# One core, a streaming encoder layer: additions of squares on VectorE, and background steps moved out of the v projection

## The chip, the cores and the metric

The program runs on one core of a Trainium2 chip. The metric is the device time of one execution in microseconds (us). The kernel before takes 2237.66 us, the median of three runs that lie between 2231.12 and 2242.47.

## The reference

One layer works on a prompt of 2048 tokens and a sample of 64 tokens, each with its own conditioning vector. The model width is 1024, the feed-forward width 2816.

```python
mod = c_act @ w_ada + b_ada                       # six vectors: sh1, sc1, gt1, sh2, sc2, gt2
h = rmsnorm(x, g1) * (1 + sc1) + sh1
u, q, k, v, o, gates = split(h @ w_in)            # 512 columns each, and 8 gates
pool_out = pool_mixer(u)                          # causal means over 2, 4, 8, 16 rows, 4 groups
hs = mlstm(q, k, v, gates)                        # 4 heads, chunks of 64 rows
hs = headnorm(hs) * sigmoid(o)
x = x + gt1 * (concat(pool_out, hs) @ w_out)
h2 = rmsnorm(x, g2) * (1 + sc2) + sh2
conv = causal_depthwise_conv3(h2 @ w_up)          # a and g, 2816 columns each
x = x + gt2 * ((silu(g) * a) @ w_down)
y = rmsnorm(x, g_final)
```

All data are float32. The final states of the pooling, the memory and the convolution are outputs too.

## The kernel before

The work has two halves. The **attention half** goes through four token groups of 512 columns (the fourth has 576, with the sample). Channels lie on the partitions, tokens along the free dimension. A float32 product is made from three passes of rounded pieces: a weight or an activation is split into a high part (ScalarE, `act.activation(..., AF.Copy)`, line 359) and the rest (VectorE, a subtraction, line 362). Weights that were split in group 0 are written to memory (`hl_kept`) and in groups 1 to 3 are read back whole (line 348), in pieces of 512 KB. The **feed-forward half** goes through three groups of 704 columns and uses sums of up-projection weights (`wsum`) that the attention half has to prepare.

In each attention group the stages are: `proj_v` (the v projection with the gates, line 1038), then for each of four heads the q, k and o projections (`proj_qko`, each one `gemm` of 24 matmuls, line 415) with the previous head's memory work (`lstm`, lines 1176 to 1254) placed between their matmuls, then four u projections with the pooling mixer, then the output projection (`outproj`), whose rows go to `x2d` and into a sum of squares.

Work that belongs to later stages is written as Python generators in five lists `bg[0]` to `bg[4]`. `tick(i)` lets the first generator of list i take one step; the places of `tick` in the matmul loops set where in the program that step's instructions stand. Four kinds of step matter here.

- **Modulations**, `ada(m, False)` in `bg[3]`, one vector of 1024 values for each of groups 1, 2 and 3 (`gt1` is made in group 0). Sixteen steps each multiply one 128 x 512 piece of `w_ada` with the conditioning vectors and add it up on VectorE (lines 194 and 196), and issue the load of a later piece (line 181), three pieces ahead, into one of four `raw` tiles. Then a few matmuls (lines 204, 211) turn the sums into columns.
- **Weight sums**, `up_sums` in `bg[4]`, over groups 1 to 3: 44 units of 512 KB. A unit is loaded by two transfers (line 801), four additions on VectorE (lines 824, 825, 827, 828) turn it into the sums, and one transfer (line 811) stores it. Each unit takes four steps. There are four tiles, so the load of unit i + 2 reuses the tile of unit i - 2 and has to wait until that was stored.
- **The norm of the next group**, `norm1` in `bg[1]`: ScalarE squares each of the eight row blocks (line 846) and GpSimd adds them up (line 848). In the last group `norm_h` (lines 675 to 695) stands in its place and prepares the feed-forward half's input.
- **The second norm's sum**, `sq_acc` in `outproj`: after each of the eight output rows (line 578 adds the residual, line 580 stores it) ScalarE squares it (line 449) and GpSimd adds it (line 450).

In the first part of group 0 and in the feed-forward half the order of PE, ACT, DVE and POOL is the program's own. Elsewhere a scheduler may issue an instruction ahead of its place once its inputs and tiles are there; transfers marked with `keep_in_program_order` (those of `up_sums` among them) keep their order among each other. Nearly all transfers are issued by one queue, SP, in order: a transfer that waits for a tile or for its data holds the ones behind it. Each engine's own instructions run in order as well.

Of the kernel before, what the change touches and what calls it, by code (L numbers as in the profile page):

```python
# [12 lines left out]
ALU = mybir.AluOpType  # L13
# [46 lines left out]
def tile_layer(ctx: ExitStack, tc: tile.TileContext, xT, vecs, cst, rst, rowv, w_mod, w_ada, w_qkou, w_v, w_pool,  # L60
# [39 lines left out]
    def tick(i=0):  # L100
        q = bg[i]
        while q:
            try:
                next(q[0])
                return
            except StopIteration:
                q.pop(0)
# [297 lines left out]
    def gemm(ps, W, mv, o, ks=None, order=None, late=None, ups=(1, 3, 4, 6)):  # L405
        order = order or list(range(len(mv)))
        ks = ks or order
        for k in ks:
            if late is not None and k == late:
                drain(0, 2)  # L410
            at = order.index(k)
            U = W.at(at // 4)
            for pi, (a, b) in enumerate(PASSES):
                for bi, (lo, hi) in enumerate(o.blks):
                    pe.matmul(ps[bi][:, :hi - lo], U[:, a, k % 4 * P:(k % 4 + 1) * P], mv[k][:, b, lo:hi],  # L415
                              start=(at == 0 and pi == 0), stop=(k == order[-1] and pi == 2))
            if at in (1, 2, 4, 6, 7):
                tick(0)
            if at in ups and not quiet:
                tick(4)  # L420
            if at == 3 and o.last and not spare:
                tick(1)
            if at == 4 and not quiet and not spare:
                tick(3)
            if spare and at in (1, 3, 4, 6):
                tick(1)
        for i in (1, 3):
            tick(i)
        for gen in list(bg[2]):
            if next(gen, 0) == 0:  # L430
                bg[2].remove(gen)
# [12 lines left out]
    def sq_acc(ssum, src, T, first):  # L444
        if first:
            act.activation(ssum[:, :T], src, AF.Square)
        else:
            s = scr()
            act.activation(s[:, :T], src, AF.Square)
            pool.tensor_tensor(out=ssum[:, :T], in0=ssum[:, :T], in1=s[:, :T], op=ALU.add)  # L450

    def ssum_tile():
        return sp.tile([P, TMAX], F32, tag="ssum", name="ssum", bufs=1)
# [154 lines left out]
    class Sums:  # L608
# [14 lines left out]
        def load(self, nm):  # L623
            for j in range(2):
                t = self.make(nm, j)
                r = 0
                for v in t:
                    b, n = r % 2, v.shape[1]
                    nc.sync.dma_start(out=v.bitcast(F32), in_=Bd[BN.index(nm), 2 * j + r // 2, :, b:b + n])
                    r += n  # L630
# [158 lines left out]
    if True:  # L789
# [6 lines left out]
        def up_sums():  # L796

            def load(f, c):
                w = a1.tile([P, 4, 256], F32, tag="w4", name="w4", bufs=4)
                for i in range(2):  # L800
                    tc.keep_in_program_order(nc.sync.dma_start(out=w[:, 2 * i:2 * i + 2, :], in_=w_up[NF * i + f].rearrange(
                        "p (h c) -> p h c", h=2)[:, :, c:c + 256]))
                return w
            todo = [(f, c) for f in range(NF) for c in (0, 256)]
            pin = tc.keep_in_program_order
            nx = [load(*todo[0]), load(*todo[1])]
            done = []

            def store():
                f, c, w = done.pop(0)  # L810
                pin(nc.sync.dma_start(out=wsum[f, :, :, c:c + 256], in_=w))
            yield
            yield
            for i, (f, c) in enumerate(todo):
                w = nx.pop(0)
                yield
                if i + 2 < len(todo):
                    nx.append(load(*todo[i + 2]))
                if done:
                    store()  # L820
                yield

                a0, a1_, g0, g1 = (w[:, i, :] for i in range(4))
                pin(dve.tensor_tensor(out=g1, in0=g0, in1=g1, op=ALU.add))
                pin(dve.tensor_tensor(out=g0, in0=a0, in1=g0, op=ALU.subtract))
                yield
                pin(dve.tensor_tensor(out=a0, in0=g1, in1=a0, op=ALU.subtract))
                pin(dve.tensor_tensor(out=a1_, in0=a1_, in1=a0, op=ALU.subtract))
                done.append((f, c, w))
                yield  # L830
            store()

# [10 lines left out]
        def norm1(o, xs, box):  # L843
            ssum = ssum_tile()
            for k, x in enumerate(xs):
                tc.keep_in_program_order(act.activation(x if k else ssum[:, :o.T], x, AF.Square))
                if k:
                    pool.tensor_tensor(out=ssum[:, :o.T], in0=ssum[:, :o.T], in1=x, op=ALU.add)
                if k > 0:
                    yield  # L850
            rs = sm.tile([P, 5], F32, tag="rs", name="rs")
            yield from rstd_rows(ssum, o, rs)
            yield
            yield
            yield from bcast(rs, o, box)
# [168 lines left out]
        def proj_v(o, h, cols):  # L1024
            nt = len(o.chunks)
            va = a1.tile([P, 5, NH, 129], F32, tag="va", name="va")
            pool.memset(va[:, :, :, 128:129], 1.0)
            gt = sm.tile([P, 5, 8], F32, tag="gt", name="gt")

            def part(hv, kh, tis, ps, W):  # L1030
                cols = VC[hv]
                tick(4)
                for ti in tis:
                    lo, n, s = o.chunks[ti]
                    for k4 in range(4):
                        U = W.at(k4 // 2)
                        for pi, (a, b) in enumerate(PASSES):
                            pe.matmul(ps[ti][:n, :cols], h[4 * kh + k4][:, b, lo:lo + n],  # L1038
                                      U[:, a, k4 % 2 * cols:(k4 % 2 + 1) * cols],
                                      start=(kh == 0 and k4 == 0 and pi == 0),  # L1040
                                      stop=(kh == 1 and k4 == 3 and pi == 2))
                    if hv == 1 or ti % 2:
                        tick(0)
                    if ti % 2 == 0:
                        tick(3)
                tick(1)

            def out(hv, tis, ps):
                for ti in tis:
                    n = o.chunks[ti][1]  # L1050
                    if hv == 1:
                        dve.tensor_copy(gt[:n, ti, :], ps[ti][:n, 256:264])
                    act.activation(va[:n, ti, 2 * hv:2 * hv + 2, 0:128],
                                   ps[ti][:n, :256].rearrange("p (h v) -> p h v", v=128), AF.Copy)

            for hv in (1, 0):
                if o.g == 0:
                    out(hv, range(4), ps_v[1 - hv])
                else:
                    ps = [mm_ps() if ti < 4 else m2_ps() for ti in range(nt)]  # L1060
                    for kh in range(2):
                        part(hv, kh, range(nt), ps, Row())
                    out(hv, range(nt), ps)
                if hv == 1:
                    bg[0].append(gate_rows(o, gt, cols))
            return va
# [80 lines left out]
        def evac(o, ps, dst, fn, **kw):  # L1147
            for bi, (lo, hi) in enumerate(o.blks):
                act.activation(dst[:, lo:hi], ps[bi][:, :hi - lo], fn, **kw)

        def proj(o, h):
            W = Row()
            ps = [mm_ps() for _ in o.blks]
            gemm(ps, W, h, o)
            return ps

        def proj_qko(o, h):
            q = a2.tile([P, TMAX], F32, tag="q", name="q")
            evac(o, proj(o, h), q, AF.Copy)
            k = a2.tile([P, TMAX], F32, tag="k", name="k")  # L1160
            evac(o, proj(o, h), k, AF.Copy, scale=HD ** -0.5)
            th = a2.tile([P, TMAX], F32, tag="th", name="th", bufs=1)
            evac(o, proj(o, h), th, AF.Tanh, scale=0.5)
            return q, k, th

        def lstm(o, hd, qko, va, cols, mix):
# [158 lines left out]
        for o in groups:  # L1325
# [2 lines left out]
                bg[4].append(up_sums())  # L1328
            if o.g > 0:
                bg[3].append(ada(2 + o.g, False))  # L1330
            if o.g == 0:
                with tc.manual_schedule(engines={ET.PE, ET.Activation, ET.DVE, ET.Pool}):
                    ps_v = first()
                    small_inputs()
                    cols = []
                    va = proj_v(o, h, cols)
            else:
                cols = []
                va = proj_v(o, h, cols)
# [518 lines left out]
```

## Time and profile before

| what | us |
|---|---|
| median of three runs | 2237.66 |
| the profiled execution's own time | 2240.48 |
| its span, first to last instruction | 2238.7 |
| TensorE (PE) busy, whole span | 2196.5 |
| VectorE (DVE) busy | 1577.7 |
| ScalarE (ACT) busy | 1002.1 |
| GpSimd (POOL) busy | 284.2 |
| group 0 | about 0 to 220 |
| group 1: v; q, k, o; u; output (about) | from 220, 245, 341, 369 |
| group 2: v; q, k, o; u; output | from 405, 429, 530, 559 |
| group 3: v; q, k, o; u; output | from 595, 630, 748, 783 |
| feed-forward half | from 827 to the end |

The mean granted TensorE clock was 0.994. In a row of the timeline the first number is the start, the second how long the group of instructions ran, and the bracket at the end says how long the engine had been idle and for what. In a row of the waits the three numbers are the total, the count and the longest. In a row by group the numbers are the busy time, the mean of one instruction in ns, and the idle time before them. "DMA" in a stage table is the mean busy share of the core's 16 DMA engines.

### The profile page before, as it was taken

What the parts mean: (1) busy time and instruction counts of PE and PEld (TensorE: products, weight loads), DVE (VectorE), ACT (ScalarE), POOL (GpSimd) and SP (SyncE); (2) the same over time, 40 slices, a digit from 0 to 9 for tenths busy, and PEclk for the clock granted to TensorE, in tenths of its full rate; (3) what the DMA queues carried; (4) which work ended last, traced back from release to release, by engine and by line L of the source; (5) the groups of instructions that cost most, each with busy time, mean ns of one, the idle gap of its engine ahead of it and who ended that gap; (6) DMA issues with size and microseconds to landing.
All of it is one profiled execution on the core that took longest, in us unless ns stands there. A gap on an engine that the chain in (4) does not pass through costs nothing.

```text
span 2238.7 us, 38008 instructions
## 1 busy us (share of the span) xinstructions
PE 2196.5 (98%) x13720; PEld 2082.8 (93%) x13720; DVE 1577.7 (70%) x2860; ACT 1002.1 (45%) x1992; POOL 284.2 (13%) x524
## 2 busy tenths in 40 slices
PE   8999999999999999999999999999999999999998
PEld 6778888878898999999999999999999999999997
DVE  4868668667755688687868677687757685757474
ACT  3544335234234356464636445445435353435254
POOL 0122012111200130010100110000001210101012
PEclk9999999999999999999999999999999999999999
DMA  9967986997888477556746964556458554353442
GB/s 351 328 231 244 342 296 230 316 305 249 272 293 273 155 241 250 191 194 240 227 157 214 300 226 165 201 187 224 142 171 267 192 201 160 114 174 123 144 151 79
DMA packets 276444, 493.52 MB, mean 220 GB/s; under 512 B 24952, under 2 KB 103416, under 8 KB 276256
## 3 DMA queue, kind: packets, MB, share of 16 engines
q1 hardware_dynamic: 266784, 468.77, 62.4%
q10 hardware_dynamic: 9472, 22.32, 2.6%
q8 instruction: 108, 1.77, 0.3%
q14 instruction: 80, 0.66, 0.1%
HBM read 382.77 MB, written 108.22 MB: 219 GB/s over the span
## 4 chain that ended last, share of the span: by engine, by line
PE 83%; DMA 8%; DVE 5%; issue 2%; ACT 1%; SPq 1%; POOL 0%; POOLq 0%; DVEq 0%; ACTq 0%
PE mm L1443 38%; PE mm L1709 22%; PE mm L415 17%; DMA raw<-w_ada 2%; PE mm L1038 1%; DMA wsum<-w 1%; DMA wt<-wsum 1%; DMA wt<-hl_kept 1%; DMA hl_kept<-wt 1%; DVE acc L196 1%; DMA w<-w_ada 1%; PE m L1222 1%; PE mm L969 1%; PE m L1221 1%; PE m L1302 1%
## 5 line engine op out<-in xcount | busy, mean ns | idle before, releaser
L1443 PE MATMUL mm<-hx,wt 128*128 128x352 f32 x5544 | 886.2, 321 | 5.8 <-ACT wt L359 3.7
L1443 PEld LDWEIGHTS mm<-hx,wt 128*128 128x128 f32 x5544 | 880.7, 188 | 7.0 <-ACT wt L359 4.3
L1709 PE MATMUL mm<-av,wt 128*128 128x352 f32 (+2 forms) x3168 | 508.1, 321 | 0.0
L1709 PEld LDWEIGHTS mm<-av,wt 128*128 128x128 f32 x3168 | 502.7, 188 | 1.8 <-DVE x L1724 0.3
L415 PE MATMUL mm<-hl,wt 128*128 128x512 f32 (+2 forms) x1920 | 399.8, 361 | 4.9 <-DMA wt<-hl_kept 3.8
L362 DVE TENSOR_TENSOR wt<-raw,wt 128x512 fp32r<-128x512 f32 (+3 forms) x494 | 309.3, 642 | 90.6 <-ACT wt L359 85.5
L415 PEld LDWEIGHTS mm<-hl,wt 128*128 128x128 f32 x1920 | 316.6, 190 | 54.7 <-issue 8.5
L359 ACT ACTIVATE wt<-raw 128x512 fp32r<-128x512 f32 (+3 forms) x494 | 271.1, 570 | 189.0 <-PE mm L1709 81.0
L1724 DVE SCALAR_TENSOR_TENSOR x<-mm,MOD,x 128x352 f32<-128x352 f32 (+4 forms) x224 | 106.4, 525 | 114.8 <-PE mm L1709 114.8
L415 PE MATMUL mm<-mx,wt 128*128 128x512 f32 (+2 forms) x960 | 185.7, 353 | 1.5 <-DVE wt L362 1.3
L415 PEld LDWEIGHTS mm<-mx,wt 128*128 128x128 f32 x960 | 158.7, 188 | 26.6 <-DVE wt L362 1.5
L1431 DVE SCALAR_TENSOR_TENSOR tg<-eg,V,tg 128x704 f32<-128x704 f32 (+1 forms) x132 | 125.6, 952 | 45.6 <-ACT tg L1426 43.2
L362 DVE TENSOR_TENSOR wt<-wt 128x512 fp32r<-128x512 f32 x176 | 122.6, 697 | 45.5 <-ACT wt L359 45.5
L359 ACT ACTIVATE wt<-wt 128x512 fp32r<-128x512 f32 x176 | 110.1, 626 | 74.0 <-DMA wt<-wsum 65.7
L1431 DVE SCALAR_TENSOR_TENSOR ta<-ea,V,ta 128x704 f32<-128x704 f32 (+1 forms) x132 | 125.6, 952 | 8.5 <-ACT ta L1426 6.2
L1566 DVE TENSOR_TENSOR av<-tg,av 128x704 fp32r<-128x704 f32 (+4 forms) x112 | 62.1, 588 | 47.7 <-ACT av L1558 47.5
L196 DVE SCALAR_TENSOR_TENSOR acc<-raw,CA,acc 128x512 f32<-128x512 f32 x84 | 62.4, 775 | 41.2 <-DMA raw<-w_ada 41.2
L1537 ACT ACTIVATE tg<-tg 128x704 f32<-128x704 f32 (+1 forms) x66 | 52.4, 794 | 79.1 <-DVE tg L1431 79.1
L1451 DVE TENSOR_TENSOR eg<-mm,u 128x352 f32<-128x352 f32 x154 | 70.1, 467 | 22.8 <-ACT u L1506 11.2
L1491 ACT ACTIVATE u<-mm 128x352 f32<-128x352 f32 x66 | 30.5, 462 | 120.2 <-PE mm L1443 82.5
L1038 PE MATMUL mm<-wt,hl 128*128 128x256 f32 (+1 forms) x576 | 71.4, 282 | 2.5 <-DVE scr L578 2.5
L1038 PEld LDWEIGHTS mm<-wt,hl 128*128 128x128 f32 x576 | 69.3, 188 | 3.6 <-DVE scr L578 2.7
(281 smaller groups left out, 2030.5 us busy)
## 6 DMA issues: line engine op xcount, KB each, us to landing
wt<-hl_kept SPq DMA_DIRECT2D x108, 512.0 KB, 6.0
raw<-w_up SPq DMA_DIRECT2D x198, 256.0 KB, 3.1
wt<-wsum SPq DMA_DIRECT2D x176, 256.0 KB, 4.1
wt<-wsplit SPq DMA_DIRECT2D x88, 512.0 KB, 4.0
raw<-w_down SPq DMA_DIRECT2D x96, 256.0 KB, 2.9
w<-w_up SPq DMA_DIRECT2D x88, 256.0 KB, 4.1
wsum<-w SPq DMA_DIRECT2D x44, 512.0 KB, 4.3
wsplit<-wt SPq DMA_DIRECT2D x44, 512.0 KB, 4.8
```

Source lines behind the costliest of these rows:

```text
L196: dve.scalar_tensor_tensor(out=acc[s], in0=w, scalar=CA[:, k, s:s + 1], in1=acc[s], op0=ALU.mult, op1=ALU.add)
L359: act.activation(u.w[:, 0, :u.n], u.raw[:, :u.n], AF.Copy)
L362: dve.tensor_tensor(out=u.w[:, 1, :u.n], in0=u.raw[:, :u.n], in1=u.w[:, 0, :u.n].bitcast(F32), op=ALU.subtract)
L415: pe.matmul(ps[bi][:, :hi - lo], U[:, a, k % 4 * P:(k % 4 + 1) * P], mv[k][:, b, lo:hi], start=(at == 0 and pi == 0), stop=(k == order[-1] ...
L1038: pe.matmul(ps[ti][:n, :cols], h[4 * kh + k4][:, b, lo:lo + n], U[:, a, k4 % 2 * cols:(k4 % 2 + 1) * cols], start=(kh == 0 and k4 == 0 and ...
L1431: dve.scalar_tensor_tensor(out=t[:, :E], in0=ext[:, j:j + E], scalar=wc(j, f), in1=t[:, :E], op0=ALU.mult, op1=ALU.add)
L1443: pe.matmul(ps[:, :FH], U[:, a, kc * P:(kc + 1) * P], Bo.at(nm, kc, b), start=(first and kc == 0 and pi == 0), stop=(kc == 3 and pi == 2), ...
L1451: dve.tensor_tensor(out=ext[:, d:d + b - a], in0=ps[:, a:b], in1=u[:, a:b], op=ALU.add)
L1537: act.activation(self.tg[:, :E], self.tg[:, :E], AF.Silu)
L1566: dve.tensor_tensor(out=cut(1), in0=self.of_tg(cut(0), a, b), in1=cut(0).bitcast(F32), op=ALU.subtract)
L1709: pe.matmul(ps[i][:, :hi - lo], U[:, a, k % 4 * P:(k % 4 + 1) * P], av[k](b, lo, hi), start=(k == 0 and (a, b) == PASSES[0]), stop=(k == n ...
L1724: dve.scalar_tensor_tensor(out=x3[n][:, a:b], in0=ps[i][:, a - lo:b - lo], scalar=gt2(n, s), in1=x3[n][:, a:b], op0=ALU.mult, op1=ALU.add)
```

## The change

- `sq_acc` and `norm1` add the squares on VectorE, not on GpSimd (28 and 21 additions). The feed-forward half's own additions of squares stay on GpSimd.
- `proj_v` no longer steps the weight sums (one step in each of its four parts) and the modulations (two steps in each part, three in group 3).
- In groups 1 to 3 the modulation's generator takes its first step (three loads) before `proj_v`; after that each q, k and o projection steps it after the third and the sixth of its eight k blocks (indices 2 and 5) and at its end, not at index 4 and its end.
- The o projection steps the weight sums five times (also at index 7), the q and k projections four times as before.
- In `up_sums` the store of the unit before now comes one step later, right ahead of this unit's first additions, and the load of unit i + 2 comes after this unit's last additions, not ahead of its first.

```diff
@@ gemm
-            if at == 4 and not quiet and not spare:
+            if at in ((2, 5) if o.g else (4,)) and not quiet and not spare:
                 tick(3)
@@ sq_acc
-            pool.tensor_tensor(out=ssum[:, :T], in0=ssum[:, :T], in1=s[:, :T], op=ALU.add)
+            dve.tensor_tensor(out=ssum[:, :T], in0=ssum[:, :T], in1=s[:, :T], op=ALU.add)
@@ up_sums
                 w = nx.pop(0)
                 yield
-                if i + 2 < len(todo):
-                    nx.append(load(*todo[i + 2]))
+                yield
                 if done:
                     store()
-                yield
 
                 a0, a1_, g0, g1 = (w[:, i, :] for i in range(4))
                 pin(dve.tensor_tensor(out=g1, in0=g0, in1=g1, op=ALU.add))
...
                 pin(dve.tensor_tensor(out=a1_, in0=a1_, in1=a0, op=ALU.subtract))
                 done.append((f, c, w))
+                if i + 2 < len(todo):
+                    nx.append(load(*todo[i + 2]))
                 yield
@@ norm1
-                    pool.tensor_tensor(out=ssum[:, :o.T], in0=ssum[:, :o.T], in1=x, op=ALU.add)
+                    dve.tensor_tensor(out=ssum[:, :o.T], in0=ssum[:, :o.T], in1=x, op=ALU.add)
@@ proj_v, part
                 cols = VC[hv]
-                tick(4)
                 for ti in tis:
...
                     if hv == 1 or ti % 2:
                         tick(0)
-                    if ti % 2 == 0:
-                        tick(3)
                 tick(1)
@@ proj, proj_qko
-        def proj(o, h):
+        def proj(o, h, ups=(1, 3, 4, 6)):
             W = Row()
             ps = [mm_ps() for _ in o.blks]
-            gemm(ps, W, h, o)
+            gemm(ps, W, h, o, ups=ups)
...
-            evac(o, proj(o, h), th, AF.Tanh, scale=0.5)
+            evac(o, proj(o, h, (1, 3, 4, 6, 7)), th, AF.Tanh, scale=0.5)
@@ loop over groups
             if o.g > 0:
                 bg[3].append(ada(2 + o.g, False))
+                tick(3)
```

## The prediction

> **What bounds the kernel now.** I read the page's busy times and chain first, then TensorE's waits in the attention half of groups 1 to 3, then a table by stage, then the instructions around each longer wait.
>
> ```profile
> PE 2196.5 (98%) x13720; PEld 2082.8 (93%) x13720; DVE 1577.7 (70%) x2860; ACT 1002.1 (45%) x1992; POOL 284.2 (13%) x524
> PE 83%; DMA 8%; DVE 5%; issue 2%; ACT 1%; SPq 1%; POOL 0%; POOLq 0%; DVEq 0%; ACTq 0%
> ```
>
> TensorE bounds nearly everywhere. No matmul is added or removed, so the change can only win or lose TensorE's waits. Those in groups 1 to 3 (line that waited, what it waited for, total, times, longest):
>
> ```profile
> PE mm L415 <- DMA wt<-hl_kept: 3.8, 2, 3.2
> PE m L1252 <- DVE sf L1237: 2.9, 1, 2.9
> PE mm L1038 <- DVE scr L578: 2.5, 1, 2.5
> PE m L477 <- DVE scr L471: 1.1, 2, 0.7
> PE m L1252 <- DVE nd L1241: 0.7, 1, 0.7
> PE m L1222 <- DVE at L1201: 0.6, 1, 0.6
> ```
>
> Stages (length, then busy time of PE, PEld, DVE, ACT, POOL, then granted clock, DMA share, GB/s):
>
> ```profile
> 220.00:245.00 25.00, 24.61 (x210) 23.84 (x209) 11.71 (x24) 5.81 (x11) 2.31 (x2) 1.00 1.03 370
> 245.00:345.00 100.00, 99.21 (x520) 80.82 (x520) 65.35 (x139) 34.95 (x101) 15.81 (x14) 1.00 0.90 305
> 441.00:458.00 17.00, 13.72 (x66) 11.17 (x66) 10.37 (x26) 4.85 (x16) 0.00 (x0) 0.90 0.99 326
> 559.00:595.00 36.00, 36.00 (x158) 29.28 (x157) 33.10 (x56) 14.16 (x26) 9.49 (x6) 1.00 0.80 257
> 700.00:725.00 25.00, 21.66 (x140) 20.56 (x141) 12.28 (x30) 8.40 (x24) 0.83 (x1) 0.86 0.83 258
> 800.00:830.00 30.00, 27.26 (x201) 26.55 (x200) 29.89 (x64) 18.44 (x40) 12.47 (x4) 1.00 0.71 236
> ```
>
> The v projection (first row) has DMA full and VectorE half empty; q, k and o (second) have DMA at 0.90. After a wait of about 3 us the granted clock drops: 0.90 over 17 us costs 0.10 x 17 = 1.7 us, and 0.86 over 25 us costs 3.5 us. The second row held only short waits and kept 1.00.
>
> **Steps of the weight sums and the order of their loads and stores.** No work is removed: each group loses its four steps in v and gains one in each of four o projections. In group 2 v's steps end in this:
>
> ```profile
> SPq L811 <- DVE w L824: 7.9, 1, 7.9
> 437.92 0.56 SPq L811 DMA_DIRECT2D wsum<-w  x1
> 439.24 0.90 SPq L348 DMA_DIRECT2D wt<-hl_kept  x1
> 444.19 1.19 PE L415 MATMUL mm<-hl,wt 128*128 128x512 f32 x2 [3.15 <-DMA wt<-hl_kept]
> SPq L801 <- DMA wsum<-w: 69.3, 31, 6.1
> ```
>
> SP stands 7.9 us at a store whose additions are queued on VectorE behind the gate rows; the weights behind it on SP are issued late; TensorE waits 3.15 us. Afterwards the store comes three steps behind its last addition, not two, and no step lies beside v. **3.2 of wait and 1.7 of clock: -4.9** (between 0 and -4.9).
>
> The last row is the next load, which reuses the tile of the store before last: it held SP 69.3 us in 31 waits, 2.2 us each. The load moves from four steps behind that store to five, and one step is about 2 us (four to a projection, 12 projections in the 100 us row), so most of such a wait goes. The load keeps seven steps, some 14 us, before its additions. In group 3 this queue also feeds the loads of the next norm:
>
> ```profile
> 701.34 0.58 DVE L675 SCALAR_TENSOR_TENSOR mx<-mx,G,mx 128x352 f32<-128x352 f32 x1 [2.69 <-DMA mx<-x2d]
> 702.67 0.52 PE L1252 MATMUL m<-ident,nd 128*128 128x128 f32 x3 [2.88 <-DVE sf L1237]
> ```
>
> L675 waits for a load that SP issued late, L1237 stands behind it on VectorE, and TensorE waits for L1237 and then L1241: 2.9 + 0.7. I take half of it, because the load still shares SP with weights and sums; a half-sized wait is one of those after which the clock stayed at 1.00, so the 3.5 us go: **-1.8 - 3.5 = -5.3** (0 to -7.1).
>
> **Steps of the modulations (L181, L194, L196).** Of a group's calls of them the 8 in v (12 in the last group) go, and each q, k or o projection issues three, not two. Three loads still go out ahead of v.
>
> ```profile
> 601.25 0.75 DVE L196 SCALAR_TENSOR_TENSOR acc<-raw,CA,acc 128x512 f32<-128x512 f32 x1 [6.04 <-DMA raw<-w_ada]
> 602.71 0.51 PE L1038 MATMUL mm<-wt,hl 128*128 128x264 f32 x2 [2.46 <-DVE scr L578]
> ```
>
> Such a step stood 6.04 us at its load, with the last output row's L578 behind it; TensorE needs that bank. With the steps elsewhere this wait and those for L471 in v go: **-2.5 - 1.1 = -3.6** (0 to -3.6). What is late next in v is only its own weights. Now all 16 steps stand in front of the heads' small instructions on VectorE. The nearest row is L1222's 0.6 us in the head of group 1, where 9 such steps ran; 16 make it 1.1, or 0.5 more, in each of three groups: **+1.5** (0 to +25, the second rival).
>
> **49 additions of squares, GpSimd to VectorE.** 28 are in the output projection, 21 in the next group's norm; 14 have 576 columns. The same addition on VectorE is L933.
>
> ```profile
> L933 DVE TENSOR_TENSOR scr<-scr 128x512 f32<-128x512 f32 x6 | 3.8, 685 | 0.5 <-ACT scr L928 0.5
> L1241 DVE TENSOR_TENSOR nd<-nd,sf 128x512 f32<-128x512 f32 (+1 forms) x20 | 20.3, 1014 | 16.8 <-POOL sf L1239 16.8
> 91.54 0.69 DVE L1241 TENSOR_TENSOR nd<-nd,sf 128x512 f32<-128x512 f32 x1 [0.92 <-POOL sf L1239]
> 464.66 1.43 POOL L848 TENSOR_TENSOR ssum<-ssum,mx 128x576 f32<-128x576 f32 x1
> 464.70 1.94 DVE L1241 TENSOR_TENSOR nd<-nd,sf 128x512 f32<-128x512 f32 x1 [1.12 <-POOL sf L1239]
> L825 DVE TENSOR_TENSOR w<-w 128x256 f32<-128x256 f32 x44 | 22.6, 515 | 0.6
> L824 DVE TENSOR_TENSOR w<-w 128x256 f32<-128x256 f32 x44 | 18.3, 416 | 3.0 <-DMA w<-w_up 3.0
> L722 DVE TENSOR_TENSOR hx<-fscr,hx 128x352 fp32r<-128x352 f32 x28 | 14.8, 567 | 0.0
> L725 DVE TENSOR_TENSOR fscr<-fscr 128x352 f32<-128x352 f32 x4 | 3.3, 824 | 1.5 <-DMA fscr<-h2d 1.5
> ```
>
> They cost 35 x 0.685 + 14 x 0.77 = 34.8 us of VectorE. But a VectorE instruction that meets one of them on GpSimd now waits it out: L1241 takes 0.69 us alone and 1.94 beside L848. Its 20 should take about 16 x 0.69 + 4 x 0.28 = 12.2 us (the four have a quarter of the columns or less) and take 20.3; L825 takes 0.1 us more than its twin L824, 44 times. These two lines lose 12.5 us already, so VectorE's net load grows by far less than 34.8, and nothing in the outputs (36 us, 33.1 busy, some 7 of them modulation steps that now go later) becomes bound. Each addition now waits for its square on ScalarE with VectorE's queue behind it; ScalarE is half idle and needs 0.6 us, which the outputs' free VectorE time covers; uncovered, it is 28 x 0.6 us of VectorE.
>
> Two places reach TensorE. In group 0:
>
> ```profile
> 88.97 1.26 DVE L1237 SCALAR_TENSOR_TENSOR sf<-sf,sq 128x4 f32<-128x4 f32 x1
> 111.48 1.29 DVE sf L1237
> PE m L1252 <- DVE nd L1241: 3.0, 3, 1.5
> ```
>
> In two heads an L1237 of four columns took 1.26 and 1.29 us beside such an addition, against 0.69 for the 512 columns of a free L1241, and L1241 comes right behind it. TensorE's waits for L1241 were 3.0 us in the whole run (third row) and 0.7 in groups 1 to 3, so 2.3 here, and both are of the size that L1237 lost. **-2.2** (0 to -2.3). And at 800 to 830 VectorE is full (29.89 of 30): seven additions cost 5.4 us, against 4 x (0.82 - 0.52) + 28 x (0.567 - 0.515) = 2.7 that L725 and L722 lose now, taking 0.52 as their time alone: **+2.7** (0 to +5.4).
>
> **Sum**: -4.9 - 5.3 - 3.6 + 1.5 - 2.2 + 2.7 = -11.8 us. Against the profiled execution (2240.5, span 2238.7) that is 2228.7; it lies 2.8 above the median of 2237.7, so the forecast is **2225.9 us**, 0.5% faster.
>
> **Rivals.** *First, the steps don't leave.* Instructions are issued ahead of their place in the program:
>
> ```profile
> L181 SPq DMA_DIRECT2D raw<-w_ada x48: 328/527/1462, 198.2 to 619.0; - x48
> DMA to landing us min/median/max: 2.5/5.8/9.0
> ```
>
> Group 1's modulation loads start at 198.2, 22 us ahead of v. If the later steps are drawn forward as far, they still run inside v: -3.6 and -5.3 are lost, +1.5 too, and 2225.9 + 7.4 = 2233.3. Against it: a step that stands 25 us later, drawn forward by 22, lands in v's end at the earliest. Chance 0.15.
>
> *Second, slower: the heads' VectorE queue stops at late modulation loads.* Per projection of 8.3 us (100 us row) there would be two weight pieces, one sum loaded and stored, and three modulation pieces:
>
> ```profile
> wt<-hl_kept SPq DMA_DIRECT2D x108, 512.0 KB, 6.0
> w<-w_up SPq DMA_DIRECT2D x88, 256.0 KB, 4.1
> raw<-w_ada SPq DMA_DIRECT2D x48, 256.0 KB, 5.8
> ```
>
> 1.05 + 1.05 + 0.79 MB in 8.3 us is 348 GB/s, close to the 370 of the full row. It decides once a load takes longer than its lead of three steps, 8.3 us: the longest took 9.0. If so in the two heads that the 16 steps fill, each wait costs TensorE 2.5 us, as L578's did, and 1.7 of clock: 3 groups x 2 x 4.2 = +25.2, with the -5.3 not gained: -11.8 + 5.3 - 1.5 + 25.2 = +17.2, or 2254.9. The median landing of 5.8 speaks against it. Chance 0.23. The Trainium skill (DMA: Bandwidth & Descriptors, Specifications) gives about 358 GB/s as a core's HBM limit, by which 348 would all but decide it; the 370 here disagrees.
>
> *Third, VectorE pays the additions in full.* Then 2.2 isn't gained and the end costs 5.4: -6.9, or 2230.8. It needs blocked instructions to find other things to wait for. Chance 0.10. The Trainium skill (Perfetto Trace Analysis, Optimizing Scalar/DVE Operations) says that a saturated VectorE may be relieved by GpSimd, though the two share a read port and it might not help; its first half is this rival, and L1241's 1.94 is the second.
>
> **Numbers.** The forecast has 0.52, and with it faster by over 0.5% (11.2 us, about what a measurement of this kernel can tell from no change); rivals one and three make 0.25 within it; rival two makes 0.23 slower. Low end: all terms at their best, -17.9, less 6 for the runs' own spread: 2214, and 2211 with the smaller waits. High end: rival two, 2255.
>
> **What would show it.** Right: no L848 or L450 on GpSimd, L1241 near 0.69 us throughout; L801's wait for stores far below 69 us; no 3 us wait for hl_kept at q's start, and granted clock 1.00 there; no wait for L578 in v. Wrong: L196 standing for w_ada between the heads' instructions with L1252 or L1222 late by 2 us and more, or L362 late near the end of the half.

## The result

The kernel after takes **2230.91 us** (median of 22 runs, 2222.37 to 2235.95), the kernel before 2237.64 (22 runs, 2231.12 to 2242.47). The ratio is 0.9966, with a 95% interval of 0.9958 to 0.9974: the change saves about 7 us, 0.3%, where 12 were forecast. The direction is as forecast, and the saving is clear of the noise; but it is smaller than the 0.5% that the prediction, with a chance of 0.52, had it exceed.

The profiled execution of after took 2230.7 us (span 2228.9, granted clock 0.994). The engines in its page:

```profile
PE 2193.3 (98%) x13720; PEld 2080.2 (93%) x13720; DVE 1573.4 (71%) x2909; ACT 1004.7 (45%) x1992; POOL 197.5 (9%) x475
```

VectorE runs 49 instructions more and is busy 4 us *less* (1577.7 before). GpSimd lost 86.7 us. TensorE still bounds, so the waits of TensorE tell the story again. In 200 to 840 us (line that waited, for what, total, times, longest):

```profile
PE mm L1441 <- DVE wt L362: 5.0, 1, 5.0
PE mm L415 <- DMA wt<-hl_kept: 2.8, 1, 2.8
...
PE mm L415 <- DVE scr L578: 0.6, 2, 0.4
```

(Behind the diff, lines have moved up by one to three: L1441, L1249, L1238 and L1234 are L1443, L1252, L1241 and L1237 of before; L822 to L826 are L824 to L828.) Gone are the waits for L1237, for L1241, for L578 in v, for L471 and for L1201. The wait for `hl_kept` stayed, and one for L362 grew from 1.2 us to 5.0. The stages, in the columns of the table shown for before:

```profile
220.00:245.00 25.00, 25.00 (x214) 24.34 (x213) 11.40 (x21) 6.06 (x11) 1.01 (x1) 1.00 0.96 322
441.00:458.00 17.00, 14.25 (x72) 11.28 (x71) 11.19 (x23) 3.43 (x14) 0.00 (x0) 0.90 0.89 304
627.00:752.00 125.00, 125.00 (x928) 117.73 (x926) 74.34 (x194) 49.26 (x159) 10.82 (x18) 1.00 0.82 269
800.00:830.00 30.00, 22.78 (x142) 21.85 (x141) 21.36 (x47) 10.87 (x22) 2.07 (x2) 0.89 0.54 187
```

The third row is all heads of group 3: TensorE busy 125.00 of 125.00 us, clock 1.00. The second, q of group 2, looks much as it did before, clock 0.90 included. In the first, v of group 1, VectorE is as busy as before (11.40 us, 11.71 then): what was to leave v has not shown up as room. The fourth is the new loss: TensorE idle for 7 of 30 us, the clock at 0.89, and VectorE busy for 21.36 us where it was full before. It is not short of time there; it waits.

The queue of SP and the groups of VectorE:

```profile
SPq L801 <- DMA wsum<-w: 19.2, 14, 2.5
L1238 DVE TENSOR_TENSOR nd<-nd,sf x20: 284/693/695, 93.1 to 743.6; 128x512 f32<-128x512 f32 x16, 64x128 f32<-64x128 f32 x4
L1238 DVE TENSOR_TENSOR nd<-nd,sf 128x512 f32<-128x512 f32 (+1 forms) x20 | 12.2, 611 | 17.0 <-POOL sf L1236 17.0
L450 DVE TENSOR_TENSOR ssum<-ssum,scr 128x512 f32<-128x512 f32 (+1 forms) x28 | 19.8, 706 | 6.5 <-ACT scr L449 4.9 <-ACT ssum L446 1.5
L848 DVE TENSOR_TENSOR ssum<-ssum,mx 128x512 f32<-128x512 f32 (+1 forms) x21 | 14.9, 709 | 0.3 <-ACT mx L846 0.2
```

SP's waits of the loads (L801) for the stores fell from 69.3 us to 19.2. L1238 (second row: minimum, median and maximum in ns) never takes longer than 695 ns: no instruction of it is blocked any more, and its 20 take 12.2 us, not 20.3. L823, the L825 of before, takes 18.4 us in all where it took 22.6. The additions themselves cost 19.8 + 14.9 = 34.7 us.

### The profile page after: what moved, and what is told of

Same layout as the page of the kernel before. It is cut to its first block, busy times and chain, and to the rows that moved or that the text cites. A ratio compares the mean times of both kernels' runs of the same rounds, so it can differ in the third digit from the quotient of the medians.

```text
span 2228.9 us, 37979 instructions
## 1 busy us (share of the span) xinstructions
PE 2193.3 (98%) x13720; PEld 2080.2 (93%) x13720; DVE 1573.4 (71%) x2909; ACT 1004.7 (45%) x1992; POOL 197.5 (9%) x475
## 4 chain that ended last, share of the span: by engine, by line
PE 60%; DMA 1%; DVE 1%; issue 0%; ACT 0%; POOL 0%; POOLq 0%; SPq 0%; ACTq 0%; DVEq 0%
PE mm L1441 37%; PE mm L1707 22%; DMA wt<-wsum 1%; DMA yT<-x 0%; ACT tg L1424 0%; DVE tg L1429 0%; DMA wt<-wsplit 0%; DMA x<-x2d 0%; ACT wt L359 0%; PE m L1595 0%; DVE ta L1429 0%; ACT ta L1424 0%; PE m L1621 0%; DVE hx L722 0%; DVE wt L362 0%
## 5 line engine op out<-in xcount | busy, mean ns | idle before, releaser
L1441 PE MATMUL mm<-hx,wt 128*128 128x352 f32 x5544 | 887.5, 321 | 8.8 <-DVE wt L362 5.0
L1441 PEld LDWEIGHTS mm<-hx,wt 128*128 128x128 f32 x5544 | 881.7, 188 | 10.3 <-DVE wt L362 5.2
L362 DVE TENSOR_TENSOR wt<-raw,wt 128x512 fp32r<-128x512 f32 (+3 forms) x494 | 307.2, 638 | 88.5 <-ACT wt L359 78.7
L359 ACT ACTIVATE wt<-raw 128x512 fp32r<-128x512 f32 (+3 forms) x494 | 271.2, 570 | 191.3 <-PE mm L1707 81.6
L415 PE MATMUL mm<-mx,wt 128*128 128x512 f32 (+1 forms) x960 | 186.0, 353 | 2.2 <-DVE wt L362 1.6
L362 DVE TENSOR_TENSOR wt<-wt 128x512 fp32r<-128x512 f32 x176 | 121.9, 693 | 45.5 <-ACT wt L359 45.1
L359 ACT ACTIVATE wt<-wt 128x512 fp32r<-128x512 f32 x176 | 110.0, 626 | 69.9 <-DMA wt<-wsum 64.0
L196 DVE SCALAR_TENSOR_TENSOR acc<-raw,CA,acc 128x512 f32<-128x512 f32 x84 | 60.7, 746 | 30.3 <-DMA raw<-w_ada 30.3
L1480 ACT ACTIVATE s<-mm 128x352 f32<-128x352 f32 x66 | 30.6, 463 | 90.0 <-PE mm L1441 89.7
```

Of the source, the lines that this page charges most:

```text
L196: dve.scalar_tensor_tensor(out=acc[s], in0=w, scalar=CA[:, k, s:s + 1], in1=acc[s], op0=ALU.mult, op1=ALU.add)
L359: act.activation(u.w[:, 0, :u.n], u.raw[:, :u.n], AF.Copy)
L362: dve.tensor_tensor(out=u.w[:, 1, :u.n], in0=u.raw[:, :u.n], in1=u.w[:, 0, :u.n].bitcast(F32), op=ALU.subtract)
L1441: pe.matmul(ps[:, :FH], U[:, a, kc * P:(kc + 1) * P], Bo.at(nm, kc, b), start=(first and kc == 0 and pi == 0), stop=(kc == 3 and pi == 2), ...
```

## The experiments

Three things were open. Which part of the change gained what? Where does the new loss at the end of the attention half come from: from the last group's seven additions, which give VectorE another order of instructions there, or from something that the moved steps brought? And why did the wait in group 2 stay: because steps of the sums, drawn ahead out of the first head, still hold SP, or for another reason? Each run below is compared with before on the same chip. Times saved are worked out from the ratio; the difference of the medians differs from them by up to 1.7 us.

### The additions alone

Before, with the two lines of additions on VectorE and nothing else of the change.

```diff
-            pool.tensor_tensor(out=ssum[:, :T], in0=ssum[:, :T], in1=s[:, :T], op=ALU.add)
+            dve.tensor_tensor(out=ssum[:, :T], in0=ssum[:, :T], in1=s[:, :T], op=ALU.add)
...
-                    pool.tensor_tensor(out=ssum[:, :o.T], in0=ssum[:, :o.T], in1=x, op=ALU.add)
+                    dve.tensor_tensor(out=ssum[:, :o.T], in0=ssum[:, :o.T], in1=x, op=ALU.add)
```

> The kernel before, with only the 49 additions of squares moved to VectorE. Theory A (the additions are worth little in sum: they end group 0's two waits of 2.3 us and the short waits in groups 1 to 3, and give it back at the end of the attention half, where the changed kernel's TensorE waits 5.0 us for L362): between -3 and +5 us against before. Theory B (the additions are the whole gain, because GpSimd no longer stops VectorE): -5 to -9 us, and the long wait at the end of the half isn't there, since it comes from the steps that moved. Either way L1241 near 0.69 us throughout and SP's wait of L801 for stores still near 69 us.

2235.44 us, ratio 0.9986 (0.9977 to 0.9995): 3.1 us faster. Its waits of TensorE in 200 to 840 us, and one of SP's queue:

```profile
PE mm L415 <- DMA wt<-hl_kept: 4.3, 1, 4.3
PE m L1252 <- DVE sf L1237: 3.0, 1, 3.0
PE mm L1443 <- DVE wt L362: 2.6, 1, 2.6
SPq L801 <- DMA wsum<-w: 73.7, 31, 5.1
...
800.00:830.00 30.00, 25.20 (x163) 24.10 (x162) 26.45 (x59) 13.83 (x30) 0.00 (x0) 0.90 0.63 201
```

The last row is the stage at the end. The additions leave SP's queue (73.7 us) and the two long waits of groups 2 and 3 standing (4.3 us for `hl_kept`, where before had 3.2, and 3.0). The wait for L578 in v of group 3 is gone, though no step, load or store was moved. At the end the wait for L362 has grown from 1.2 to 2.6 us, and the clock of that stage is 0.90 where before had 1.00, which is 3 us more. So the additions by themselves already make much of the loss at the end; the rest of it needs the moved steps too.

### The steps and the load order alone

After, with both kinds of additions back on GpSimd (the two lines above reversed).

> The changed kernel with the 49 additions back on GpSimd; steps and order of loads and stores as changed. Theory A: -6 to -12 us against before, as good as the whole change or better: no wait for L578 in v of group 3, no wait at L1252 in group 3's heads, group 0's waits of 2.3 us back, and no 5 us wait at the end of the half. Theory B: -2 to +2 us, and the 5 us wait at the end stays.

2236.28 us, 0.9985 (0.9976 to 0.9994): 3.4 us faster. The rows of TensorE in 200 to 840 us that differ, and SP's:

```profile
PE m L1249 <- DVE nd L1238: 2.3, 2, 1.8
PE mm L1037 <- DVE scr L578: 2.2, 2, 1.4
SPq L801 <- DMA wsum<-w: 25.3, 13, 4.9
```

The gain lies between the two expectations, and neither had the waits right: the 5 us at the end is gone (0.3 us for the feed-forward half's products, 2.5 for the output projection's, 1.3 there before), but L578 is late. SP is freed here as in after. But with the additions on GpSimd, VectorE is late in the heads (L1238) and at the start of v (L578), where after has nothing. The two halves of the change give 3.1 and 3.4 us, and together about 7.

### Only the last group's seven additions back on GpSimd

```diff
-            dve.tensor_tensor(out=ssum[:, :T], in0=ssum[:, :T], in1=s[:, :T], op=ALU.add)
+            (pool if T == TMAX else dve).tensor_tensor(out=ssum[:, :T], in0=ssum[:, :T], in1=s[:, :T], op=ALU.add)
```

This is after with 7 of its 49 additions elsewhere; only the last group has T == TMAX.

> The changed kernel with the seven additions of the last group's output projection back on GpSimd, all else as changed. Theory A (VectorE's order near the end, with the additions in it, puts L362 late): the 5.0 us wait of the feed-forward half's first products for L362 falls to the 1 to 3 us of before, and the half clock after it goes: 4 to 8 us faster than the changed kernel, -11 to -15 against before. Theory B (the wait comes from weight sums that land late, whoever adds): no more than 2 us from the changed kernel.

2225.71 us, 0.9937 (0.9922 to 0.9951): 14.1 us faster than before, and by the two ratios 0.3% faster than after. The timeline of the end (start, length; in brackets the idle time ahead and for what), first of after:

```profile
814.42 0.63 ACT L359 ACTIVATE wt<-wt 128x512 fp32r<-128x512 f32 x1 [1.39 <-DMA wt<-wsum]
815.47 1.40 DVE L722 TENSOR_TENSOR hx<-fscr,hx 128x352 fp32r<-128x352 f32 x3 [2.91 <-ACT hx L715]
816.78 1.06 DVE L578 SCALAR_TENSOR_TENSOR scr<-mm,MOD,scr 128x256 f32<-128x256 f32 x3
818.19 0.69 DVE L362 TENSOR_TENSOR wt<-raw,wt 128x512 fp32r<-128x512 f32 x1
818.93 1.54 PE L1441 MATMUL mm<-hx,wt 128*128 128x352 f32 x4 [4.98 <-DVE wt L362]
```

then of this kernel, with its stage row:

```profile
811.69 0.68 DVE L362 TENSOR_TENSOR wt<-raw,wt 128x512 fp32r<-128x512 f32 x1
812.29 1.06 DVE L578 SCALAR_TENSOR_TENSOR scr<-mm,MOD,scr 128x256 f32<-128x256 f32 x3
812.43 1.75 PE L1441 MATMUL mm<-hx,wt 128*128 128x352 f32 x9 [1.23 <-DVE wt L362]
...
800.00:830.00 30.00, 27.48 (x185) 26.92 (x184) 23.02 (x44) 12.61 (x24) 12.81 (x9) 1.00 0.75 239
```

and of before:

```profile
828.01 0.68 DVE L362 TENSOR_TENSOR wt<-raw,wt 128x512 fp32r<-128x512 f32 x1
828.61 1.05 DVE L578 SCALAR_TENSOR_TENSOR scr<-mm,MOD,scr 128x256 f32<-128x256 f32 x3
```

In before and in this kernel the split of the first up weights (L362) stands *ahead* of the last output rows (L578). In after it stands behind them, and behind L722, which waits 2.91 us for ScalarE's L715; ScalarE had been waiting for `wsum` from memory. The same instructions but for the seven additions, in another order on one engine, make 5 us of wait and, at a clock of 0.89 over 30 us, 3.3 us more. The first two experiments agree: with the additions alone L362 starts at 826.26 us, behind the L578 of 824.85; with the additions on GpSimd it starts at 824.88, ahead of the L578 of 825.48. So the seven additions are the cause, by way of the order. How long the wait gets depends on the moved steps too: with the additions alone it was 2.6 us, together with the steps 5.0. A second profile of after, unchanged, was taken to see whether this was one late transfer.

> The changed kernel once more, for its profile. If the wait of about 5 us for L362 at the end of the attention half belongs to the order of instructions, it is there again, between 4 and 6 us; if it was one late transfer of that execution, it is below 2 us.

```profile
PE mm L1441 <- DVE wt L362: 4.7, 1, 4.7
PE mm L415 <- DMA wt<-hl_kept: 2.4, 1, 2.4
```

Both waits are there again (2235.12 us, one run): they belong to the kernel's order, not to chance.

### The load and store order alone

Before, with only `up_sums` changed: the store a step later, the load behind the unit's additions.

```diff
                 yield
-                if i + 2 < len(todo):
-                    nx.append(load(*todo[i + 2]))
+                yield
                 if done:
                     store()
-                yield
...
                 done.append((f, c, w))
+                if i + 2 < len(todo):
+                    nx.append(load(*todo[i + 2]))
```

> The kernel before, with only the places of the weight sums' loads and stores changed. Theory A (L801's wait for stores is what makes SP late): SP's wait of L801 falls from 69 us below 30, the wait at L1252 in group 3's heads (2.9 us, with half clock after it) goes, the wait for L578 in v of group 3 (2.5 us) stays: -3 to -8 us against before. Theory B (the steps' places decide, not the order): -1 to +2 us and the wait at L1252 stays.

2234.33 us, 0.9984 (0.9973 to 0.9995): 3.6 us faster. SP's row, then the first of TensorE's in 200 to 840 us:

```profile
SPq L801 <- DMA wsum<-w: 2.5, 2, 1.8
PE mm L415 <- DMA wt<-hl_kept: 4.5, 2, 2.3
```

One reordering takes SP's 69.3 us at the loads down to 2.5, and the wait of 2.9 us for L1237 in group 3 is gone, with the half clock behind it. This confirms the mechanism of the second term of the forecast, alone, but not its size. SP now stands longer at the stores (L811 for L826: 43.2 us in 15; for the same line, L828 of before, 28.2 in 13). Of the 4.5 us for `hl_kept`, 2.3 are in q of group 2, and the other 2.3 are new, in the first head of group 3:

```profile
643.06 4.14 PE L415 MATMUL mm<-hl,wt 128*128 128x256 f32 x18 [2.26 <-DMA wt<-hl_kept]
```

From 643.8 to 647.1 us the clock is 0.50. This new wait of 2.3 us and its 1.7 us of clock take back 4.0 of the 6.4 us (2.9 and 3.5) that were gained in the heads of group 3.

It also tells on the third term. TensorE's wait for L578 at the start of group 3's v, which was expected to stay, is gone here too, though no step was moved. The timeline of VectorE there, of this kernel:

```profile
593.37 0.75 DVE L578 SCALAR_TENSOR_TENSOR scr<-mm,MOD,scr 128x512 f32<-128x512 f32 x1 [2.29 <-PE mm L415]
598.74 0.75 DVE L196 SCALAR_TENSOR_TENSOR acc<-raw,CA,acc 128x512 f32<-128x512 f32 x1 [4.28 <-DMA raw<-w_ada]
```

and of after:

```profile
591.81 0.75 DVE L578 SCALAR_TENSOR_TENSOR scr<-mm,MOD,scr 128x512 f32<-128x512 f32 x1 [2.52 <-PE mm L415]
598.96 2.74 DVE L196 SCALAR_TENSOR_TENSOR acc<-raw,CA,acc 128x512 f32<-128x512 f32 x4 [4.95 <-DMA raw<-w_ada]
```

In both a modulation step still stands 4 to 5 us at its load inside v. But the last output row now runs ahead of it, where in before it was queued behind. That is not the work of this edit alone: with only the additions moved, and with only the places of the steps changed, the last L578 runs early as well (at 595.53 and 596.87 us), and the wait is gone.

### Only the places of the steps

Before, with the steps in v, q, k and o moved as in the change, but the old order in `up_sums` and the additions on GpSimd.

```diff
-            if at == 4 and not quiet and not spare:
+            if at in ((2, 5) if o.g else (4,)) and not quiet and not spare:
...
-                tick(4)
...
-                    if ti % 2 == 0:
-                        tick(3)
...
+            evac(o, proj(o, h, (1, 3, 4, 6, 7)), th, AF.Tanh, scale=0.5)
...
+                tick(3)
```

> The kernel before, with only the places of the steps changed (no step of sums and modulations in v, three modulation steps in each q, k and o projection, one more step of the sums in each o projection); order of loads and stores and the additions as before. Theory A (the steps' places take the wait for L578 in v of group 3, 2.5 us, and the order of loads and stores has its own gain): -2 to -5 us, L578's wait gone, SP's wait of L801 still over 50 us and the wait at L1252 in group 3 still there. Theory B (what steps_only gained came from the order alone): -1 to +2 us.

2243.66 us, 1.0012 (1.0002 to 1.0023): 2.7 us *slower* than before, and worse than either theory had it. SP's row, TensorE's in 200 to 840 us, and the first stretch of the heads of group 3:

```profile
SPq L801 <- DMA wsum<-w: 80.1, 34, 7.4
PE m L1249 <- DVE nd L1238: 2.7, 2, 1.5
PE m L1218 <- DVE SN L1212: 2.2, 1, 2.2
627.00:700.00 73.00, 69.16 (x487) 64.62 (x486) 41.17 (x112) 27.96 (x87) 2.37 (x3) 0.95 0.83 267
```

The wait for L578 in v is gone, but the denser steps make SP's queue worse (80.1 us), and VectorE is late in the heads: almost 4 us of TensorE idle in this stretch and 0.05 x 73 = 3.7 us of clock. VectorE itself stands there for late loads: 10.79 us ahead of an L824 at 650.31 and 4.04 ahead of one at 689.00, both for `w_up`, and further on 4.48 us ahead of the L675 at 723.76, for `x2d`. TensorE's waits of 1.6, 2.0 and 2.2 us end right behind these. Moving the steps is no gain by itself. It pays in company: steps and order together (the second experiment) give -3.4, and with the additions off GpSimd the heads of group 3 have no wait at all.

### The earlier groups' output additions back on GpSimd too

After, with all 28 additions of `sq_acc` on GpSimd and the 21 of the norm on VectorE (one line differs from after). Against the version with seven on GpSimd it tells whether the other 21 matter.

> The changed kernel with all 28 additions of the output projection back on GpSimd; the 21 of the next group's norm stay on VectorE. Theory A (only the norm's additions meet instructions that TensorE waits for, those of the heads, and only the last seven of the output's reach TensorE, on the other side): as fast as pool_at_end within 3 us, -11 to -16 us against before, L1238 (the old L1241) at 0.69 us throughout. Theory B (in the outputs too GpSimd's additions hold VectorE up so that TensorE waits): 4 us or more slower than pool_at_end.

2231.16 us, 0.9959 (0.9945 to 0.9973), 0.2% or about 5 us slower than with seven on GpSimd; the runs of the two do not overlap (2229.67 to 2234.49 and 2221.80 to 2226.58). In 200 to 840 us:

```profile
PE mm L1037 <- DVE scr L578: 1.8, 2, 1.3
```

L578 at the start of v is late again, as in the kernel with all additions on GpSimd; in both, as in before, it runs behind the step that waits for its load. Its 1.8 us are only a part of the 5; short waits in the gates and heads (L1207 1.2 us, L1072 0.6, L1218 0.5) are more of it. So with the steps and loads as changed, the additions in the earlier groups' outputs do belong on VectorE; at the end they do not. One rule for all places would miss that.

### The sums kept out of the first head's q

The version with seven additions on GpSimd, and the first head's q takes no step of the sums; each k takes one more.

```diff
-            evac(o, proj(o, h), q, AF.Copy)
+            evac(o, proj(o, h, (1, 3, 4, 6) if hd else ()), q, AF.Copy)
-            evac(o, proj(o, h), k, AF.Copy, scale=HD ** -0.5)
+            evac(o, proj(o, h, (1, 3, 4, 6, 7)), k, AF.Copy, scale=HD ** -0.5)
```

> The kernel of pool_at_end (the changed one, last seven additions on GpSimd), in which the first q projection of a group takes no step of the weight sums and each k projection takes one more, so that the count stays. Theory A (in group 2 the sums' stores and loads still stand on SP in front of the weights while VectorE works through the gate rows, as before, only shifted from v to the first head): the wait for hl_kept of 2.3 us and the half clock after it go: 2 to 5 us faster than pool_at_end, -16 to -19 us against before. Theory B (the wait comes from the modulation loads and the full DMA): no change within 1.5 us, the wait stays.

2220.86 us, 0.9914 (0.9898 to 0.9931): 19.3 us faster than before, and faster than every other kernel here. What held SP, first in after:

```profile
432.80 0.43 DVE L822 TENSOR_TENSOR w<-w 128x256 f32<-128x256 f32 x1
433.26 0.68 DVE L1118 TENSOR_TENSOR RHL<-scr,RHL 4x512 fp32r<-4x512 f32 x1
436.09 0.56 SPq L811 DMA_DIRECT2D wsum<-w  x1
440.48 0.53 SPq L348 DMA_DIRECT2D wt<-hl_kept  x1
447.45 2.04 PE L415 MATMUL mm<-hl,wt 128*128 128x512 f32 x5 [2.75 <-DMA wt<-hl_kept]
```

then in this kernel, with its stage row:

```profile
430.05 0.68 DVE L1118 TENSOR_TENSOR RHL<-scr,RHL 4x512 fp32r<-4x512 f32 x1
437.33 0.53 SPq L348 DMA_DIRECT2D wt<-hl_kept  x1
438.21 0.42 DVE L822 TENSOR_TENSOR w<-w 128x256 f32<-128x256 f32 x1
441.11 0.56 SPq L811 DMA_DIRECT2D wsum<-w  x1
...
441.00:458.00 17.00, 17.00 (x94) 14.23 (x93) 14.84 (x38) 6.07 (x20) 1.17 (x1) 1.00 0.91 302
```

In after the additions of the sums (L822) still lie between the gate rows (L1118 is the last of these), drawn forward out of the first q; the store waits for them, and the weights wait behind the store. Here the gate rows run first, the weights are issued ahead of the store, TensorE has no wait in the stretch, and the clock is 1.00. In the profile of the kernel that this one was made from, the wait was 2.31 us and the clock 1.00 already, so the row shows 2.3 of the 5 us between the two; where the rest is was not settled.

The store's wait alone does not fix the size: with the steps moved and the old store order there was no `hl_kept` wait in this stretch, and with steps and order but the additions on GpSimd it was 1.1 us. TensorE was idle there for 2.6 and 3.1 us all the same, in short waits for other rows, at a clock of 1.00. How many weight pieces SP had issued before it stopped may be what decides; that was not tried.

## Why the prediction was right, and where it wasn't

**What bounds.** It held: no matmul changed, and what was won and lost is TensorE's waits and the clock behind them. The half clock after a wait was as priced: 0.90 over 17 us again in group 2, 0.89 over 30 us at the end.

**The steps of the sums in group 2 (-4.9): failed.** The wait fell from 3.2 to 2.8 us, with the same clock, about -0.4. The step of the prediction that failed is "no step lies beside v": the additions did not come later than the gate rows, since they are issued ahead of their place. That was the first rival's mechanism, which I had put on the modulations only. The steps of the sums had only to be drawn from the first q into the gate rows just ahead of it. Kept out of that q, they take the wait with them, as was forecast: the last kernel is 0.2% faster than the one it was made from, though its profile shows only 2.3 us of this as the wait.

**SP's queue freed, group 3 (-5.3): right, at the better end.** I let half of the two waits go; both went, and the clock with them: 2.9 + 0.7 + 3.5 = 7.1. The order alone did it to L1237, and L801's wait fell by far more than "most" (2.5 us when alone). Alone it also brought the new wait for `hl_kept` in the same heads; in the whole change those heads have none.

**Modulation steps out of v (-3.6): right amount, wrong reason.** L578's 2.5 and L471's 1.1 are gone, against 0.4 more for L578 in the output projections (0.6, 0.2 before). But the steps hardly left. L196 inside group 3's v (length of the stage, VectorE's busy time for this line and count), in before and in after:

```profile
595.70:629.90 34.20, 14.58 (x19) 1.00 0.92 324
...
591.60:621.80 30.20, 10.02 (x14) 1.00 0.91 304
```

Nineteen became fourteen: the first rival, in place; with only the places of the steps changed there were still nineteen. I had let it cost -3.6 and -5.3. It cost neither, since SP is freed by the load and store order, wherever the steps run, and L578 by VectorE's order, the last L578 ahead of a step that waits long for its load. The step that failed is "with the steps elsewhere this wait goes": the steps did not go elsewhere, and the wait did not depend on it. Any one part of the change by itself (additions, load order, places) let L578 run early; places and load order together, with the additions on GpSimd, put it behind again (2.2 us in two waits). So the gain can't be put down to one of the three edits. What the traces show is the order: in the three kernels that have the wait in group 3, L578 stands behind an L196 that waits 6.04, 6.23 and 6.10 us for its load.

**Denser steps in the heads (+1.5): right only for the whole change.** After has no wait for L1201, so it is -0.6. Alone, the moved steps cost more than they gain, in group 3's heads: the second rival's place and sign, at a sixth of its price (+2.7 against +17). There VectorE stands for late loads of the sums and of the next norm, not of the modulations, with SP's queue at 80.1 us; in the whole change the freed SP and the unblocked L1238 take it back. Even the rival's condition, a load later than its lead, came once in after, in the first head of group 3:

```profile
638.61 0.75 DVE L196 SCALAR_TENSOR_TENSOR acc<-raw,CA,acc 128x512 f32<-128x512 f32 x1 [10.98 <-DMA raw<-w_ada]
```

VectorE was idle for 11 us, and TensorE, busy for 125.00 of 125.00 us in that stage, never noticed. The price of 2.5 us for each such wait was taken from a place where a row that TensorE needed stood behind it; here none did.

**Additions, VectorE's load and group 0 (-2.2): right.** 34.7 us against 34.8 worked out, 12.2 for L1241 as worked out, and the wait for it fell from 3.0 us in the whole run to 0.4. The third rival, that VectorE pays in full, is refuted by its busy time, 4 us less; that its 2230.8 us nearly is the time measured is chance. The Trainium skill (SBUF — State Buffer, Who interferes with whom) says that a VectorE instruction with two SBUF inputs and a GpSimd instruction that reads SBUF contend for a shared pair of ports, which is an exclusive lock. The trace agrees: L1241 took up to 1.94 us beside L848, and at most 0.695 with no such GpSimd addition left.

**Additions at the end (+2.7): direction right, size and mechanism wrong.** I priced VectorE as full and counted time: 5.4 us in, 2.7 out. VectorE was busy for 21.36 of 30 us. The loss is 5.0 - 1.2 = 3.8 us of wait and 3.3 of clock, 7.1 in all, because an order changed and VectorE waited for ScalarE. The upper bound of +5.4, worked out from busy time, was too low for the same reason: a changed order has no price in a table of busy times. "L362 late near the end of the half" did stand in the list of what would show it wrong.

With the waits as measured, the sum is -0.4 - 7.1 - 3.2 - 0.6 - 1.9 + 7.1 = -6.1 us (the fifth is group 0's part: 2.6 less for L1238 in the whole run, 0.7 of them counted in group 3). The medians say -6.7. The two profiled executions from which the waits are read are 9.8 us apart, so some of their difference stands in no term. In the feed-forward half before's profile has a wait of 2.3 us for L359 near 1330 us with a half clock behind it; after's has 1.4 us there and no half clock, but the second profile of after has two such waits with their half clocks again. That part varies from one execution to the next. Two terms make nearly all of the miss: 4.5 us in group 2 and 4.4 at the end; SP's queue and the heads, 1.8 and 2.1 better, give a part of it back, and v and group 0 were 0.4 and 0.3 worse.

## What to carry to other kernels

Where a scheduler may issue work ahead of its place, a step that is moved just behind a critical stretch can come back into it: read from the trace where it runs, and keep it out of the stretch behind as well. On an in-order queue a load that reuses a tile just behind that tile's store holds everything behind it, and one step more between the two was worth more here than moving the steps themselves. When work moves onto an engine, price its time by what it stops blocking as well, but look apart at the places where that engine's order feeds the next stage: seven of 49 additions were worth more where they had been.

## What the runs showed of the hardware

- Moving 34.7 us of additions onto VectorE lowered VectorE's busy time, from 1577.7 to 1573.4 us in after and to 1574.1 with nothing else changed. The prediction counted 12.5 us of blocking in two lines; all lines other than the additions together came out 38 to 39 us lower.
- The clock of 0.90 over 17 us and of 0.86 over 25 us is, in narrower windows, a clock of 0.50 for about 3.4 or 6.8 us (before: 443.9 to 447.2 and 703.4 to 710.1 us). So a wait that brings it costs about 1.7 or 3.4 us of clock.
- All eight TensorE waits of 2.6 us or more between 200 and 2200 us of the ten traces had such a stretch at their end; the shortest were 2.61 and 2.75 us. Among waits of 1.5 to 2.5 us length did not decide: in q of group 2, 2.39 us in the second profile of after was followed by a clock of 0.50 and 2.31 in the kernel with seven additions on GpSimd was not; before's 2.46 us in v of group 3 was not, and 1.85 us in the second profile of after (at 1790 us) was. The Trainium skill (TensorE: Matmul & The Clock Gate, HAM oscillation — how this bites in real kernels) gives as its rule no idle gaps above about 3.4 us; here shorter ones were enough.
